# Low parts of plain weights by a negated copy and an adding transfer

## The chip, the cores and the metric

The kernel runs on one core of a Trainium2 chip. The metric is the time of one execution on the device in microseconds (us). The engines are TensorE (PE, matmuls; its weight loads are listed as PEld), VectorE (DVE), ScalarE (ACT), GpSimd (POOL) and SyncE (SP), which here issues nearly all transfers between the chip's memory and the core.

## The reference

Two layers of a diffusion trunk over 128 context and 512 latent tokens, 640 columns in all, of width 1024. A layer is a feed-forward network (FFN), a mixer, and a second FFN, each behind a normalization that is scaled and shifted by a conditioning vector:

```python
def ffn_sublayer(x, mod, k, g, w_in, w_out):
    h = modulated_norm(x, mod, k, g)
    gt, up = jnp.split(h @ w_in, 2, axis=-1)
    return x + 0.5 * mod[:, None, 3 * k + 2] * ((jax.nn.silu(gt) * up) @ w_out)

def trunk_layer(x, mod, ...):
    x = ffn_sublayer(x, mod, 0, norm_g[0], w_ffn_in[0], w_ffn_out[0])
    h = modulated_norm(x, mod, 1, norm_g[1])
    ...  # h @ w_in, then attention, pooling and convolution groups
    x = x + mod[:, None, 5] * y
    return ffn_sublayer(x, mod, 2, norm_g[2], w_ffn_in[1], w_ffn_out[1]), k, v
```

An FFN's hidden width is 2816, so w_in has 2 x 2816 columns. The conditioning values come from one product of each layer, 1024 by 9216, with the weights w_ada. All is in float32.

## The kernel before

The activations lie with the 1024 features on partitions (eight tiles x_92 to x_99 of 128 by 640) and are worked on in two halves of 320 columns. A float32 product is made of three products in a faster format (f32r): each operand is split into a high part, which is the value rounded to that format, and a low part, which is the rest. The function mm3 (L343 to L349) multiplies wh by xh (L347), wh by xl (L348) and wl by xh (L349).

A weight tile goes through these steps. SyncE loads it into one of five raw tiles (raw, 128 by 1024; L176). ScalarE copies it to wh, which rounds it (L170). Another engine subtracts wh from raw and writes wl (L171). Both are done by split_w; its argument eng says who subtracts: GpSimd, unless the caller names VectorE. There are four wh and four wl tiles of 1024 columns, and two of 512. A raw tile is free again when wh and wl have been made of it, and SyncE's queue waits for that before it issues the next load into it.

GpSimd makes the low parts of 330 tiles: 209 of 1024 columns (w_ffn_in, w_in, w_out and part of w_ffn_out), 64 of 640 (w_ffn_out) and 57 of 512. VectorE makes those of 114 sums of weight tiles, and of the first two tiles of the kernel.

The FFNs work through 22 column blocks of the gate and up weights. In the first FFN all are plain. In each of the other three the last 19 blocks, 57 in all, are done by fast_ups: seven half products in place of eight, with sums of raw tiles made by VectorE (`add`, L641). Of such a step's tiles, the up weights (1024 columns) and half of the gate weights (512 columns) go through GpSimd, and the two sums through VectorE. ScalarE keeps partial products (part, L666), applies silu (L677, L681) and copies the high part of g (L155); VectorE makes the low part of g (L156). The down products run in five chunks between the blocks and update x (L513, VectorE). Behind each FFN or mixer, squares of x are taken by ScalarE (sq, L246), added by VectorE (ssq, L247), and a matmul with ones sums them over the partitions (mis, L370). In three of the four FFNs the conditioning weights of the next stages are loaded through the same raw tiles (L150) and used by VectorE (L306) or TensorE (L270).

The order in which each engine takes its instructions is set by the program's scheduler, from its own estimates of durations; tiles are handed over by semaphores. The low part's subtraction is this one line, with h the high part:

```python
eng.tensor_tensor(lo, raw, f32(h), op=ALU.subtract)
```

Of the kernel before, what the change touches and what calls it, by code (L numbers as in the profile page):

```python
# [12 lines left out]
AF = mybir.ActivationFunctionType  # L13
ALU = mybir.AluOpType
# [82 lines left out]
def trunk_kernel(ctx: ExitStack, tc: tile.TileContext, i: dict, o: dict):  # L97
    nc = tc.nc
# [21 lines left out]
    def f32(ap):  # L120
        return ap.bitcast(F32)
# [42 lines left out]
    def split_w(raw, nk, width, eng=nc.gpsimd):  # L164

        view = lambda t: t[:, : nk * width].rearrange("p (k c) -> p k c", k=nk)
        size, tag = (1024, "") if nk * width > 512 else (512, "s")
        h = view(whp.tile([P, size], F32R, tag="wh" + tag, name="wh", bufs=4 if tag == "" else 2))
        lo = view(wlp.tile([P, size], F32R, tag="wl" + tag, name="wl", bufs=4 if tag == "" else 2))
        nc.scalar.activation(h, raw, AF.Copy)  # L170
        eng.tensor_tensor(lo, raw, f32(h), op=ALU.subtract)  # L171
        return h, lo

    def load_raw(src, c0, width=P, raw=None):
# [7 lines left out]
    def load_w(loads, nk=KD, width=P):  # L182
        return split_w(*raw_w(loads, nk, width))

    def load_cols(src, c0, width=P):
        return split_w(*load_raw(src, c0, width))
# [364 lines left out]
    def ffn(l, f, n, hs, side, finish, nxt, first=None):  # L551
# [83 lines left out]
        def fast_weights(j):  # L635

            nk = KD // 2
            up, *_ = load_raw(w_in, DFF + j * P)
            gate, *_ = load_raw(w_in, j * P)
            a1, a2, d1, d2 = up[:, :nk, :], up[:, nk:, :], gate[:, :nk, :], gate[:, nk:, :]  # L640
            add = lambda out, x, y: nc.vector.tensor_tensor(out, x, y, op=ALU.add)  # L641
            view = lambda t: t.rearrange("p (k c) -> p k c", k=KD)
            one, two = view(sum_tile()), view(sum_tile())
            ups = split_w(up, KD, P)
            add(one[:, :nk, :], a1, d1)
            add(one[:, nk:, :], d1, d2)
            add(two[:, :nk, :], one[:, nk:, :], a1)
            add(two[:, nk:, :], two[:, :nk, :], a2)
            late = split_w(d2, nk, P)
            twos = split_w(two, KD, P, nc.vector)  # L650
            ones = split_w(one, KD, P, nc.vector)
            first = lambda w: (w[0][:, :nk, :], w[1][:, :nk, :])
            second = lambda w: (w[0][:, nk:, :], w[1][:, nk:, :])
            return {1: first(ups), 2: second(ups), 3: second(twos), 4: late, 5: second(ones), 6: first(twos), 7: first(ones)}
# [731 lines left out]
```

## Time and profile before

| | us |
|---|---|
| median of three timed runs | 2446.3 (2445.64 to 2448.29) |
| the profiled execution | 2451.2 |
| its span | 2449.4 |
| TensorE busy in it | 2326.0 |
| VectorE, ScalarE, GpSimd busy | 1627.4, 952.9, 744.3 |

The mean granted clock of TensorE was 0.978 of the full one. The stages end at about 540 us (first FFN), 775 (mixer), 1275 (second FFN), 1750 and 1987 (the same of the second layer's first FFN and mixer), and 2449. Times inside a row are counted from the start of the span. Busy times of engines overlap, so they do not add up to the span; a wait of TensorE adds to it.

### The profile page before, as it was taken

Reading aid. Unit: us, or ns where it says so; the run is one execution under the profiler, and the core shown is the slowest. Engines: PE = TensorE matmul, PEld = TensorE weight load, DVE = VectorE, ACT = ScalarE, POOL = GpSimd, SP = SyncE. Lnnn points to the kernel's source line nnn. Section 1 sums busy time; section 2 is a strip of 40 time slices with the busy share of each in tenths; the row PEclk is TensorE's granted clock in tenths of the full one; section 3 lists DMA queues with packets and bytes.
Section 4 is the critical chain, followed back from the end, with each engine's and each line's share of the span. In section 5 each row is a group of like instructions: output and inputs, shape, how many; then the busy total and the mean of one; then the engine's idle time right before and its main releaser. Section 6 shows DMA issues by size and latency. Waiting matters only on the chain.

```text
span 2449.4 us, 40825 instructions
## 1 busy us (share of the span) xinstructions
PE 2326.0 (95%) x16594; PEld 2235.4 (91%) x16594; DVE 1627.4 (66%) x2907; ACT 952.9 (39%) x1750; POOL 744.3 (30%) x383
## 2 busy tenths in 40 slices
PE   7999999989899999999989999999898989999999
PEld 6999999979877899999989999999797789999998
DVE  5757776567868757466568475575778687566673
ACT  4322221234466424343335342343444564344351
POOL 2434333333311332232322323323242133332331
PEclk9999999989999999999999999999899999999999
DMA  8535454322211444353423333333122012322221
GB/s 264 155 112 166 145 166 128 122 70 69 62 35 35 127 124 123 111 164 98 135 70 98 110 117 108 121 110 108 52 80 59 27 44 67 91 84 78 78 87 44
DMA packets 341300, 247.57 MB, mean 101 GB/s; under 512 B 25752, under 2 KB 301560, under 8 KB 341112
## 3 DMA queue, kind: packets, MB, share of 16 engines
q1 hardware_dynamic: 340932, 244.88, 33.4%
q8 instruction: 131, 2.15, 0.4%
q14 instruction: 57, 0.47, 0.1%
q10 hardware_dynamic: 180, 0.07, 0.0%
HBM read 242.04 MB, written 2.88 MB: 100 GB/s over the span
## 4 chain that ended last, share of the span: by engine, by line
PE 74%; DVE 15%; DMA 4%; ACT 3%; issue 3%; POOL 0%; ACTq 0%; SPq 0%; DVEq 0%; POOLq 0%
PE acc L347 22%; PE acc L348 21%; PE acc L349 21%; DMA raw<-in_w_ffn_in 4%; DVE sums L641 3%; DVE sums L306 2%; PE mis L270 2%; DVE ssq L247 2%; PE po L1095 1%; DVE x L513 1%; PE acc L1055 1%; PE po L349 1%; PE po L348 1%; PE mis L1106 1%; PE po L347 1%
## 5 line engine op out<-in xcount | busy, mean ns | idle before, releaser
L171 POOL TENSOR_TENSOR wl<-raw,wh 128x1024 fp32r<-128x1024 f32 (+2 forms) x330 | 715.0, 2173 | 1594.0 <-ACT wh L170 1527.6
L347 PE MATMUL acc<-h,wh 128*128 128x320 f32 (+1 forms) x2808 | 881.5, 316 | 40.0 <-ACT part L666 13.9
L348 PE MATMUL acc<-h,wh 128*128 128x320 f32 (+1 forms) x2808 | 874.8, 312 | 6.7 <-DVE h L407 3.9
L349 PE MATMUL acc<-h,wl 128*128 128x320 f32 (+1 forms) x2808 | 872.1, 311 | 0.0
L347 PEld LDWEIGHTS acc<-h,wh 128*128 128x128 f32 x2808 | 532.7, 190 | 60.8 <-ACT part L666 17.9
L170 ACT ACTIVATE wh<-raw 128x1024 fp32r<-128x1024 f32 (+2 forms) x332 | 306.4, 923 | 655.2 <-PE acc L348 483.4
L348 PEld LDWEIGHTS acc<-h,wh 128*128 128x128 f32 x2808 | 533.4, 190 | 9.7 <-DVE h L407 4.1
L349 PEld LDWEIGHTS acc<-h,wl 128*128 128x128 f32 x2808 | 533.1, 190 | 0.6 <-issue 0.6
L347 PE MATMUL acc<-g,wh 128*128 128x320 f32 x1408 | 438.9, 312 | 20.0 <-DVE x L513 20.0
L348 PE MATMUL acc<-g,wh 128*128 128x320 f32 x1408 | 437.7, 311 | 0.0
L349 PE MATMUL acc<-g,wl 128*128 128x320 f32 x1408 | 436.6, 310 | 0.0
L513 DVE SCALAR_TENSOR_TENSOR x<-acc,gate,x 128x128 f32<-128x128 f32 (+2 forms) x480 | 194.5, 434 | 258.5 <-PE acc L349 257.3
L347 PEld LDWEIGHTS acc<-g,wh 128*128 128x128 f32 x1408 | 265.8, 189 | 24.3 <-issue 11.6
L349 PEld LDWEIGHTS acc<-g,wl 128*128 128x128 f32 x1408 | 266.2, 189 | 0.2
L348 PEld LDWEIGHTS acc<-g,wh 128*128 128x128 f32 x1408 | 266.0, 189 | 0.3
L170 ACT ACTIVATE wh<-sums 128x1024 fp32r<-128x1024 f32 x114 | 120.3, 1056 | 159.6 <-PE acc L348 140.3
L156 DVE TENSOR_TENSOR g<-part,g 128x320 fp32r<-128x320 f32 x114 | 143.0, 1254 | 56.6 <-ACT g L155 56.3
L306 DVE SCALAR_TENSOR_TENSOR sums<-raw,c,sums 128x512 f32<-128x512 f32 x196 | 174.1, 945 | 9.4 <-DMA raw<-in_w_ada 9.3
L171 DVE TENSOR_TENSOR wl<-sums,wh 128x1024 fp32r<-128x1024 f32 x114 | 139.5, 1225 | 53.3 <-ACT wh L170 40.6
L641 DVE TENSOR_TENSOR sums<-raw 128x512 f32<-128x512 f32 x114 | 107.2, 975 | 55.1 <-DMA raw<-in_w_ffn_in 54.4
L641 DVE TENSOR_TENSOR sums<-sums,raw 128x512 f32<-128x512 f32 x114 | 97.2, 853 | 2.0
L347 PE MATMUL acc<-mix,wh 128*128 128x320 f32 x256 | 83.7, 327 | 13.2 <-DVE u L1021 12.7
(199 smaller groups left out, 2528.7 us busy)
## 6 DMA issues: line engine op xcount, KB each, us to landing
raw<-in_w_ffn_in SPq DMA_DIRECT2D x176, 512.0 KB, 4.0
raw<-in_w_ada SPq DMA_DIRECT2D x128, 512.0 KB, 3.8
raw<-in_w_ffn_out SPq DMA_DIRECT2D x48, 512.0 KB, 4.0
raw<-in_w_ffn_out SPq DMA_DIRECT2D x64, 320.0 KB, 3.3
raw<-in_w_in SPq DMA_DIRECT2D x20, 512.0 KB, 3.8
adaw<-in_w_ada SPq DMA_DIRECT2D x16, 512.0 KB, 10.5
raw<-in_w_in SPq DMA_DIRECT2D x16, 256.0 KB, 4.0
raw<-in_w_out SPq DMA_DIRECT2D x8, 512.0 KB, 3.5
```

Of the source, the lines that this page charges most:

```text
L156: nc.vector.tensor_tensor(lo, src, f32(h), op=ALU.subtract)
L170: nc.scalar.activation(h, raw, AF.Copy)
L171: eng.tensor_tensor(lo, raw, f32(h), op=ALU.subtract)
L247: nc.vector.tensor_tensor(ssq[:, c:e], ssq[:, c:e], sq[:, : e - c], op=ALU.add)
L270: last = nc.tensor.matmul(ps[32 * g : 32 * g + 32, 0:P], c2[:, 2 * q + k, :], r[:, k, g * P : (g + 1) * P], start=(q + k == 0), stop=(q + ...
L306: nc.vector.scalar_tensor_tensor(part[:, j, :], r[:, k, :], c, part[:, j, :], op0=ALU.mult, op1=ALU.add)
L347: nc.tensor.matmul(out, wh, xh, start=start, stop=False, skip_group_check=onto)
L348: nc.tensor.matmul(out, wh, xl, start=False, stop=False, skip_group_check=onto)
L349: return nc.tensor.matmul(out, wl, xh, start=False, stop=stop, skip_group_check=onto)
L513: nc.vector.scalar_tensor_tensor(xT[t][:, s:e], ps[:, s - a : e - a], gates[l][n][:, t, j : j + 1], xT[t][:, s:e], op0=ALU.mult, op1=ALU.add,)
L641: add = lambda out, x, y: nc.vector.tensor_tensor(out, x, y, op=ALU.add)
L1055: nc.tensor.matmul(ps[:, :w], qs[2 * c + m][:, g, self.qc], self.kk[x][:, g, :], start=(x == 0), stop=(x == 1),)
```

## The change

Where GpSimd made a low part, ScalarE now writes the negated high part into the low part's tile, and a transfer issued by GpSimd's queue adds the raw tile onto it: lo = -wh, then lo = lo + raw. The other callers, with VectorE, are as before. Five lines are added, so that the lines below L171 are numbered five higher in the changed kernel.

```diff
         h = view(whp.tile([P, size], F32R, tag="wh" + tag, name="wh", bufs=4 if tag == "" else 2))
         lo = view(wlp.tile([P, size], F32R, tag="wl" + tag, name="wl", bufs=4 if tag == "" else 2))
         nc.scalar.activation(h, raw, AF.Copy)
-        eng.tensor_tensor(lo, raw, f32(h), op=ALU.subtract)
+        if eng is nc.gpsimd:
+
+            nc.scalar.activation(lo, f32(h), AF.Copy, scale=-1.0)
+            eng.dma_start(lo, raw, accum_op=ALU.add)
+        else:
+            eng.tensor_tensor(lo, raw, f32(h), op=ALU.subtract)
         return h, lo
```

It takes 330 subtractions from GpSimd, and adds 330 copies to ScalarE and 330 transfers from on-chip memory to on-chip memory. The scheduler orders the rest anew. Two places of ScalarE's queue show it. The first is the end of the first FFN, where the squares of the last tiles of x (x_93 to x_99) stand between copies of weights for the mixer. Before:

```order
L170 ACTIVATE wh<-raw 128x1024
L246 ACTIVATE sq<-x_93 128x320
L246 ACTIVATE sq<-x_94 128x320
L170 ACTIVATE wh<-raw 128x1024
L246 ACTIVATE sq<-x_95 128x320
L246 ACTIVATE sq<-x_96 128x320
L170 ACTIVATE wh<-raw 128x1024
L246 ACTIVATE sq<-x_97 128x320
L246 ACTIVATE sq<-x_98 128x320
L170 ACTIVATE wh<-raw 128x1024
L246 ACTIVATE sq<-x_99 128x320
L356 ACTIVATE r_5379<-mis,eps 128x320
```

After, from the second of these copies on:

```order
L170 ACTIVATE wh<-raw 128x1024
L251 ACTIVATE sq<-x_95 128x320
L173 ACTIVATE wl<-wh 128x1024
L251 ACTIVATE sq<-x_96 128x320
L170 ACTIVATE wh<-raw 128x1024
L251 ACTIVATE sq<-x_97 128x320
L173 ACTIVATE wl<-wh 128x1024
L251 ACTIVATE sq<-x_98 128x320
L170 ACTIVATE wh<-raw 128x1024
L251 ACTIVATE sq<-x_99 128x320
L173 ACTIVATE wl<-wh 128x1024
L361 ACTIVATE r_5449<-mis,eps 128x320
```

A copy now stands between any two squares, and a negated copy behind the last of them. The second place is a fast step of the third FFN (the one that begins near 1645 us before). Its up weights are raw_16891 before and raw_16968 after, its half of the gate weights raw_16893 and raw_16970. Before:

```order
L170 ACTIVATE wh_16766<-sums_16748 128x1024
L666 ACTIVATE part_16721<-acc_16619 128x320
L677 ACTIVATE part_16721<-part_16721 128x320
L666 ACTIVATE part_16785<-acc_16770 128x320
L170 ACTIVATE wh_16897<-raw_16891 128x1024
L155 ACTIVATE g_16811<-part_16721 128x320
L170 ACTIVATE wh_16905<-raw_16893 128x512
L681 ACTIVATE part_16682<-part_16682 128x320
L155 ACTIVATE g_16811<-part_16682 128x320
L666 ACTIVATE part_16833<-acc_16770 128x320
```

After:

```order
L170 ACTIVATE wh_16839<-sums_16819 128x1024
L671 ACTIVATE part_16797<-acc_16695 128x320
L671 ACTIVATE part_16858<-acc_16843 128x320
L682 ACTIVATE part_16797<-part_16797 128x320
L170 ACTIVATE wh_16974<-raw_16968 128x1024
L155 ACTIVATE g_16884<-part_16797 128x320
L173 ACTIVATE wl_16975<-wh_16974 128x1024
L170 ACTIVATE wh_16983<-raw_16970 128x512
L686 ACTIVATE part_16758<-part_16758 128x320
L173 ACTIVATE wl_16984<-wh_16983 128x512
L671 ACTIVATE part_16906<-acc_16843 128x320
L155 ACTIVATE g_16884<-part_16758 128x320
```

The negated copy of the up weights stands behind the high part of g, and that of the gate weights behind a silu; the next kept part (the second last row) now comes after both.

## Rows read from the trace of the kernel before

**Rows 1.** Page, busy time by engine, and the chain that ended last by engine.

```profile
PE 2326.0 (95%) x16594; PEld 2235.4 (91%) x16594; DVE 1627.4 (66%) x2907; ACT 952.9 (39%) x1750; POOL 744.3 (30%) x383
...
PE 74%; DVE 15%; DMA 4%; ACT 3%; issue 3%; POOL 0%; ACTq 0%; SPq 0%; DVEq 0%; POOLq 0%
```

**Rows 2.** Waits of TensorE: waited for, total us, times, longest us.

```profile
PE acc L347 <- DVE x L513: 23.7, 15, 4.1
PE mis L370 <- DVE ssq L247: 22.4, 5, 8.4
PE acc L347 <- ACT part L666: 13.9, 10, 3.1
PE acc L347 <- DVE u L1021: 12.7, 2, 6.4
```

**Rows 3.** Groups of instructions by shape, GpSimd: count | busy us, mean ns | idle before.

```profile
L171 POOL TENSOR_TENSOR wl<-raw,wh 128x1024 fp32r<-128x1024 f32 x209 | 519.5, 2487 | 1287.6 <-ACT wh L170 1230.8 <-PE acc L349 28.2 <-PE acc L1055 22.4
L171 POOL TENSOR_TENSOR wl<-raw,wh 128x640 fp32r<-128x640 f32 x64 | 102.1, 1596 | 248.5 <-ACT wh L170 248.5
L171 POOL TENSOR_TENSOR wl<-raw,wh 128x512 fp32r<-128x512 f32 x57 | 95.2, 1671 | 57.9 <-ACT wh L170 48.2 <-DVE g L156 9.5
```

**Rows 4.** Groups of instructions by shape, ScalarE, copies of high parts.

```profile
L170 ACT ACTIVATE wh<-raw 128x1024 fp32r<-128x1024 f32 x211 | 223.2, 1059 | 426.6 <-PE acc L348 314.9 <-issue 94.0 <-DMA raw<-in_w_ffn_in 11.0
...
L170 ACT ACTIVATE wh<-raw 128x640 fp32r<-128x640 f32 x64 | 47.3, 740 | 197.3 <-PE acc L348 160.6 <-PE acc L349 14.9 <-issue 12.7
L170 ACT ACTIVATE wh<-raw 128x512 fp32r<-128x512 f32 x57 | 35.9, 629 | 31.2 <-DMA raw<-in_w_ffn_in 21.2 <-PE acc L348 7.9 <-issue 2.0
```

**Rows 5.** Timeline, VectorE, end of the first FFN: start us, duration us, instruction.

```profile
527.22 0.49 DVE L247 TENSOR_TENSOR ssq<-ssq,sq 128x320 f32<-128x320 f32 x1
...
538.30 2.13 DVE L247 TENSOR_TENSOR ssq<-ssq,sq 128x320 f32<-128x320 f32 x1 [0.59 <-ACT sq L246]
```

**Rows 6.** Timeline, GpSimd, same place.

```profile
537.74 2.34 POOL L171 TENSOR_TENSOR wl<-raw,wh 128x1024 fp32r<-128x1024 f32 x1 [2.40 <-ACT wh L170]
```

**Rows 7.** Timeline, TensorE: last product, next matmul; the latter in the second layer.

```profile
531.76 0.31 PE L349 MATMUL acc<-g,wl 128*128 128x320 f32 x1
...
540.48 1.44 PE L370 MATMUL mis<-ssq,ones 128*128 128x320 f32 x2 [8.41 <-DVE ssq L247]
...
1750.58 1.43 PE L370 MATMUL mis<-ssq,ones 128*128 128x320 f32 x2 [8.30 <-DVE ssq L247]
```

**Rows 8.** Stretches: length, busy us (count) by engine, granted clock, DMA share, GB/s.

```profile
545.00:550.00 5.00, 5.00 (x25) 5.00 (x25) 5.00 (x18) 3.06 (x8) 0.00 (x0) 0.66 0.03 11
550.00:560.00 10.00, 10.00 (x70) 10.00 (x70) 8.81 (x24) 6.24 (x14) 0.00 (x0) 1.00 0.00 0
```

**Rows 9.** DMA issues: count, KB each, median us to landing.

```profile
raw<-in_w_ffn_in SPq DMA_DIRECT2D x176, 512.0 KB, 4.0
...
raw<-in_w_ffn_out SPq DMA_DIRECT2D x64, 320.0 KB, 3.3
...
adaw<-in_w_ada SPq DMA_DIRECT2D x16, 512.0 KB, 10.5
```

**Rows 10.** Timeline, ScalarE, fast step of the third FFN, up weights.

```profile
1645.26 1.06 ACT L170 ACTIVATE wh<-raw 128x1024 fp32r<-128x1024 f32 x1
```

**Rows 11.** Timeline, TensorE, first product with that tile's low part.

```profile
1655.52 0.31 PE L349 MATMUL acc<-h,wl 128*128 128x320 f32 x1
```

**Rows 12.** Timeline, ScalarE, fast step of the last FFN, up weights.

```profile
2236.50 1.07 ACT L170 ACTIVATE wh<-raw 128x1024 fp32r<-128x1024 f32 x1 [0.24 <-PE acc L348]
```

**Rows 13.** Timeline, TensorE, first product with that tile's low part.

```profile
2245.55 0.31 PE L349 MATMUL acc<-h,wl 128*128 128x320 f32 x1
```

**Rows 14.** Waits of VectorE.

```profile
DVE sums L641 <- DMA raw<-in_w_ffn_in: 54.4, 29, 3.9
```

**Rows 15.** Timeline, VectorE, low parts of g in the step of rows 10.

```profile
1646.94 2.22 DVE L156 TENSOR_TENSOR g<-part,g 128x320 fp32r<-128x320 f32 x1 [0.54 <-ACT g L155]
...
1651.20 0.49 DVE L156 TENSOR_TENSOR g<-part,g 128x320 fp32r<-128x320 f32 x1 [0.54 <-ACT g L155]
```

## The prediction

> **What bounds the kernel now.** I read the page first, then the waits of TensorE, then the stretches in which it waited longest, then the DMA issues, and last the fast steps of the three later FFNs, where the changed weights are most numerous. The page shows TensorE busy for 95% of the span and holding 74% of the chain of waits; VectorE (DVE) has 15% of that chain, ScalarE 3%, and GpSimd none [rows 1]. So GpSimd's 744 us of work are worth nothing by themselves. What a change off TensorE can win is inside its idle time, and the largest entries of that are four: updates of x, sums of squares, kept partial products, and the mixer's u [rows 2]. Two of the five waits for sums of squares are long, and they stand at the end of the first FFN of each layer. In the first one the last product ends near 532.07 and the next matmul begins at 540.48, after 8.41 us; in the second, near 1750, it is 8.30 us [rows 7]. In that gap a sum of squares takes 2.13 us, whereas the same operation took 0.49 us a little earlier [rows 5], and the long one lies beside a subtraction of GpSimd that began 0.6 us before it and ended 0.35 us before it [rows 6]. The reader is to see there that VectorE, with two operands in on-chip memory, stood still until GpSimd was done. The same is seen in the fast steps: one low part of g took 2.22 us beside a subtraction and 0.49 us without one [rows 15]. There TensorE has other products to do, and does not wait.
>
> **What goes.** The 330 subtractions of 2.49, 1.60 and 1.67 us [rows 3] go, and with them the stretching of VectorE.
> - The two long waits [rows 7]: after the last product there remain the update of x, the square on ScalarE, the sum of 0.49 us and the matmul's start. The first two go over the same 320 columns as the sum, so I take 0.5 us for each of the three and some 0.8 for handing over, 2.3 us in all and 6 us less than now, each time: 12 us.
> - The other three waits for sums of squares hold 22.4 - 16.7 = 5.7 us [rows 2]; I take 4 of them.
> - In the five microseconds behind the long gap the granted clock was 0.66 on average, between the levels of 1.2 and 2.4 GHz, after TensorE had idled, and 25 matmuls were done; the next ten, at the full clock, held 70 [rows 8], 35 in five. So 10 x 0.143 = 1.4 us are lost each time; with a short gap I take them as won, 3 us for two.
> - The mixer's two waits for u have 12.7 us, and the fifteen for x 23.7 [rows 2]. VectorE is partly stretched there too; I take 3 and 2 us.
> The gains are 24 us. Everything else that VectorE wins lies beside products.
>
> **What comes in its place: copies on ScalarE.** A negated copy reads and writes what the copy of the high part does, so I price it by that: 209 x 1.059 + 64 x 0.740 + 57 x 0.629 = 305 us [rows 3, 4]. That brings ScalarE from 953 to 1258 us, 51% of the span [rows 1]. Beside it TensorE works; but ScalarE is waited for 13.9 us at kept parts [rows 2], and a longer queue makes these waits longer. In proportion to its load they grow by 13.9 x 305/953 = 4.4 us. At the ends of the FFNs the order of ScalarE now has one copy between any two squares; none stands after the last but one more negated copy, so I charge nothing more there (one copy each, 2 us, if the last square is caught behind it).
>
> **What comes in its place: 330 adding transfers.** The trace has no transfer within on-chip memory and none that adds. The nearest rows bound it: a load of 512 KB lands 4.0 us after its issue, one of 320 KB after 3.3, and the slowest kind, sixteen of 512 KB in a row, after 10.5 [rows 9]. The first two give a slope of 0.7 us for 192 KB, so 1.9 us for the bytes of a large tile and 2.1 us that do not depend on them. An adding transfer must read the raw tile and the tile it adds onto; I count its bytes twice, 2.1 + 2 x 1.9 = 5.9 us. GpSimd, which issues the transfer, is held up by VectorE in the fast steps: its subtractions of 512 columns, which stand only there, took 1.67 us, though those of 640 took 1.60 [rows 3], so 1.67 - 1.60 x 0.8 = 0.39 us more than their size asks. I add this as an allowance and take 6.3 us for a large tile, between 4.0 and 10.5, nearer to the lower end as the loads that are spaced like these transfers are there.
>
> The Trainium skill, "Collectives: The Full Stack", section "The bandwidth ceiling: the fold count and why AG ≠ RS ≠ AR", states that a transfer that reduces is slower than a copy not through its addition but through its second source, which passes through the same read ring and doubles the traffic. By it the data part is paid twice, 5.9 us; without it 4.0, and rival 1 below would lose half of its chance. No run here shows it yet.
>
> What hides it: in a fast step of the second layer's first FFN the copy of the high part ends at 1646.32 [rows 10], and the first product that needs the low part starts at 1655.52 [rows 11] (which matmul uses which tile I found by counting the products in program order). Of these 9.20 us the new order spends some 0.5 on the high part of g and 1.06 on the negated copy, and 0.1 on handing over: 7.5 us are left for the transfer. The 38 fast steps of two FFNs look like this. In the last FFN, where no modulation work lies between the products, the copy ends at 2237.57 [rows 12] and the use is at 2245.55 [rows 13]: 7.98 - 1.6 = 6.4 us, in 19 steps. At 6.3 us neither waits. The low parts of the down products and of the plain steps have at least as much, worked out in the same way.
>
> Where the lead is shorter than the new chain, TensorE pays. A low part is ready 1.06 + 6.3 - 2.49 = 4.9 us later than now. At the kernel's start and at the start of an FFN the weights have little lead; there I charge one such delay, 5 us in sum (0 to 15, if three places pay it in full).
>
> A raw tile is given back when the transfer has landed, also 4.9 us later, and SyncE's queue issues its loads in order, many of them after waiting for exactly this release. VectorE already waits 54.4 us in 29 places for a raw tile's landing [rows 14]; it would wait longer there, with the parts of the step queued behind that wait, but has 2 us fewer of stretched work in the same step [rows 15]. I set the one against the other and count zero, with bounds of -12 (the relief is used) and +40 us (about 1.4 us at each of the 29 places reach TensorE).
>
> **The sum.** 24 won, 4.4 + 5 paid: 14.6 us less than the profiled execution's 2451.2 us, 2436.6. That execution is 4.9 us above the median of the three timed runs, 2446.3, so the forecast is 2431.7, say 2431 us. A difference under 0.2% of the time, 5 us, cannot be told from no change in this kernel.
>
> **Rivals.**
> 1. The transfer lands too late (slower). It decides from 6.4 us on in 19 steps and from 7.5 on in 38. For it: the 10.5 us of loads that queue behind each other, and that GpSimd and VectorE exclude one another [rows 5, 6]. Against it: a fast step issues only two such transfers. At 9 us: 1.5 x 38 + 2.6 x 19 = 106 us, so 2431 + 106 = 2537 us; at 10.5: 3 x 38 + 4.1 x 19 = 192, 2623 us.
> 2. The issue waits for VectorE. If GpSimd is held up at each transfer as long as a sum of squares was by it, 2.13 - 0.49 = 1.64 us [rows 5] in place of 0.39, the transfer takes 7.5 us: 1.1 x 19 = 21 us, and 2452 us, no change or a little slower. The Trainium skill, "SBUF — State Buffer", section "SBUF: two separate sides", describes this as a trap: a transfer issued from GpSimd needs its descriptors written by GpSimd's cores, and a VectorE operation that takes the shared port pair keeps them out; it reports 3.1 us where 0.62 were normal. By that sentence, an estimate, 2.5 us more than 5.9 would make 8.4 us, some 70 us of waits and 2501 us. The trace agrees that the two engines exclude each other, 2.13 against 0.49 us, but shows no descriptor being written.
> 3. Late raw tiles. The 40 us of the bound above come, and the gains stay: 2431 + 40 = 2471 us. For it speak the 29 places; against it, that what VectorE makes of these tiles is needed only by products of the step after, so that only what is queued behind its wait can suffer.
> 4. The relief is hidden: squares wait behind ScalarE's copies at the ends in place of GpSimd's subtractions, 2 us at each of five waits and nothing won at x and u, which leaves some 24 - 15 - 9 = 0: 2446 us.
>
> **How the numbers follow.** The forecast has 0.46; its own range is 2410 (gains of 40, as VectorE also uses its relief in the fast steps) to 2441. Rival 1 has 0.27, rival 2 0.08, rival 3 0.11, rival 4 0.08. Faster is the forecast's 0.46 and a little of the fourth, 0.47; within 0.2% is most of the fourth and a third of the second, 0.10; slower is the rest, 0.43. The range for all must leave out no more than 2 in 10: from 2410 up to 2560, which holds rival 1 up to about 9.4 us a transfer.
>
> **What the changed profile would show.** Right: sums of squares of 0.5 us throughout, waits of TensorE for them under 3 us at the FFNs' ends with no clock below 1.0 for long after; VectorE's busy time well below 1627 us; ScalarE near 1258 us; transfers landing in 5 to 7 us; no wait of a product for a low part in the fast steps. Wrong: waits of TensorE's line for the low part's matmul (L354 after) on a transfer, some 1 to 4 us in each of 19 or 57 steps; or SyncE's loads issued so late that ScalarE and VectorE wait hundreds of microseconds for raw tiles, and through their queues TensorE at kept parts.

## The result: slower by 0.9%, the gains were there and the bodies lost more

The changed kernel takes 2466.8 us (median of five runs, 2460.5 to 2474.7) against 2446.3 for the kernel before in the same rounds; the ratio is 1.0089, with an interval of 1.0063 to 1.0115. The forecast of 2431 us had the wrong sign. The third rival had 2471 us. One execution of mix_raw6 and one of mix_raw7, two of the experiments below, took 12348.9 and 5738.8 us; their ratios leave these out.

The page of the changed kernel: busy time by engine, then the transfers' queues (packets, MB, share of the 16 engines' span), then the issues (count, KB each, median us to landing).

```profile
PE 2341.6 (95%) x16594; PEld 2250.0 (91%) x16594; DVE 1324.6 (54%) x2907; ACT 1217.4 (49%) x2080; POOL 317.4 (13%) x383
...
q1 hardware_dynamic: 340932, 244.88, 32.9%
q0 software_dynamic: 47520, 145.51, 32.7%
...
wl<-raw POOLq DMA_DIRECT2D x209, 512.0 KB, 5.2
raw<-in_w_ffn_in SPq DMA_DIRECT2D x176, 512.0 KB, 5.0
raw<-in_w_ada SPq DMA_DIRECT2D x128, 512.0 KB, 5.2
...
raw<-in_w_ffn_out SPq DMA_DIRECT2D x64, 320.0 KB, 4.2
wl<-raw POOLq DMA_DIRECT2D x64, 320.0 KB, 4.5
```

VectorE lost 303 us of work and ScalarE gained 264 [rows 1]. An adding transfer of 512 KB landed after 5.2 us, sooner than the 6.3 taken. But the queue of these transfers takes as large a share of the DMA engines (32.7%) as all loads (32.9%), and a load of 512 KB of w_ffn_in now lands after 5.0 us and not 4.0, one of 320 KB after 4.2 and not 3.3 [rows 9].

What TensorE waits for in the changed kernel (total us, times, longest):

```profile
PE acc L352 <- DVE x L518: 41.5, 13, 6.9
PE acc L352 <- ACT part L671: 24.5, 17, 3.3
PE acc L354 <- DMA wl<-raw: 15.4, 13, 4.7
...
PE mis L375 <- DVE ssq L252: 3.8, 2, 1.9
...
PE acc L352 <- DVE u L1026: 1.3, 2, 0.7
```

Against [rows 2], the sums of squares fell from 22.4 to 3.8 us and u from 12.7 to 1.3; the updates of x rose from 23.7 to 41.5, kept parts from 13.9 to 24.5, and 15.4 us for low parts are new.

Where the time went is told best by stage. Each normalization begins with a matmul that sums squares (L370, after L375), once for each half of the tokens; I cut both traces at these starts, and call the piece between the two halves an end. In us:

| | first FFN | end | mixer | end | FFN 2 | end | FFN 3 | end | mixer | end | FFN 4 | four bodies | ends and mixers |
|---|---|---|---|---|---|---|---|---|---|---|---|---|---|
| before | 519.1 | 21.4 | 219.2 | 24.5 | 474.3 | 22.5 | 448.2 | 21.4 | 220.6 | 24.5 | 453.7 | 1895.3 | 554.1 |
| after | 530.3 | 14.9 | 209.7 | 17.2 | 494.3 | 17.2 | 481.7 | 14.8 | 212.4 | 17.1 | 463.4 | 1969.6 | 503.3 |

So the ends and mixers became 51 us shorter, and the FFN bodies 74 us longer; the profiled execution, 2474.7 us, is the longest of the five.

The end of the first FFN, in the changed kernel; VectorE, then TensorE (start us, duration us, instruction, and in brackets the idle time before it and what ended it):

```profile
541.08 0.49 DVE L252 TENSOR_TENSOR ssq<-ssq,sq 128x320 f32<-128x320 f32 x1 [0.76 <-ACT sq L251]
...
544.60 0.49 DVE L252 TENSOR_TENSOR ssq<-ssq,sq 128x320 f32<-128x320 f32 x1 [0.75 <-ACT sq L251]
```

```profile
542.95 0.31 PE L354 MATMUL acc<-g,wl 128*128 128x320 f32 x1
...
545.15 1.40 PE L375 MATMUL mis<-ssq,ones 128*128 128x320 f32 x2 [1.89 <-DVE ssq L252]
```

This answers to [rows 5, 7]: no sum of squares takes more than 0.5 us, and the gap is 1.89 us in place of 8.41. The clock did not gain by it here. In the second five microseconds after that matmul, read as [rows 8], TensorE does 19 matmuls at a granted clock of 0.50, the level of 1.2 GHz; before, behind the long gap, it did 25 at 0.66:

```profile
550.00:555.00 5.00, 4.86 (x19) 4.46 (x18) 5.00 (x18) 3.29 (x9) 0.62 (x2) 0.50 1.00 239
```

The low parts of g have lost their stretch as well; all 114 in the fast steps before, then after (us in sum, mean ns of one):

```profile
L156 DVE TENSOR_TENSOR g<-part,g 128x320 fp32r<-128x320 f32 x114 | 143.0, 1254 | 56.6 <-ACT g L155 56.3
```

```profile
L156 DVE TENSOR_TENSOR g<-part,g 128x320 fp32r<-128x320 f32 x114 | 56.0, 492 | 68.5 <-ACT g L155 67.6
```

The loss is seen in a down stage of the third FFN. First SyncE's queue, GpSimd and ScalarE, then VectorE, then TensorE:

```profile
1595.86 1.88 SPq L181 DMA_DIRECT2D raw<-in_w_ffn_in  x2
```

```profile
1598.19 0.89 POOL L174 DMA_DIRECT2D wl<-raw  x1 [2.69 <-ACT part L682]
```

```profile
1604.04 0.63 ACT L170 ACTIVATE wh<-raw 128x512 fp32r<-128x512 f32 x1 [5.90 <-DMA raw<-in_w_ffn_in]
```

```profile
1598.24 0.67 DVE L518 SCALAR_TENSOR_TENSOR x<-acc,gate,x 128x128 f32<-128x128 f32 x2 [0.88 <-PE acc L354]
1604.11 0.69 DVE L646 TENSOR_TENSOR sums<-raw 128x512 f32<-128x512 f32 x1 [5.20 <-DMA raw<-in_w_ffn_in]
1604.72 0.54 DVE L518 SCALAR_TENSOR_TENSOR x<-acc,gate,x 128x320 f32<-128x320 f32 x1
```

```profile
1605.32 0.42 PE L352 MATMUL acc<-g,wh 128*128 128x320 f32 x1 [3.61 <-DVE x L518]
```

Two loads go out from 1595.86 on, an adding transfer at 1598.19; the loads are in at about 1604, after some 8 us. The 16 DMA engines are full meanwhile: their share (the last number but one; the one before it is the granted clock) is over 1.

```profile
1601.00:1606.00 5.00, 1.39 (x9) 1.13 (x9) 1.85 (x4) 1.26 (x2) 0.26 (x1) 1.00 1.12 264
```

VectorE stands at a sum of raw tiles for 5.20 us, with the update of x behind it in its queue, and TensorE waits 3.61 us for that update, since it frees the accumulator. The wait costs more than its length, as the granted clock is lower after it:

```profile
1606.00:1611.00 5.00, 5.00 (x26) 5.00 (x25) 2.63 (x7) 2.11 (x2) 1.47 (x2) 0.66 0.87 244
```

26 matmuls are done in these five microseconds at a granted clock of 0.66, between the levels of 1.2 and 2.4 GHz; 35 are done at the full one [rows 8]. Over the whole kernel TensorE's busy time rose from 2326.0 to 2341.6 us, for the same 16594 matmuls.

SyncE's queue, which waited for GpSimd's subtractions before it could load into a raw tile, now waits for the landings of adding transfers (before, then after; total us, times, longest):

```profile
SPq L176 <- POOL wl L171: 997.8, 205, 38.3
```

```profile
SPq L181 <- DMA wl<-raw: 1353.4, 222, 37.0
```

And the waits for raw tiles grew over the whole kernel, VectorE's from 54.4 us [rows 14] to the first of these rows, ScalarE's from 32.2 [rows 4] to the second:

```profile
DVE sums L646 <- DMA raw<-in_w_ffn_in: 167.0, 37, 7.8
```

```profile
ACT wh L170 <- DMA raw<-in_w_ffn_in: 178.9, 38, 12.4
```

### The profile page after: what moved, and what is told of

The parts are those of the page before. It is cut to its first block, busy times and chain, and to the rows that moved or that the text cites. A ratio compares the mean times of both kernels' runs of the same rounds, so it can differ in the third digit from the quotient of the medians.

```text
span 2472.9 us, 41585 instructions
## 1 busy us (share of the span) xinstructions
PE 2341.6 (95%) x16594; PEld 2250.0 (91%) x16594; DVE 1324.6 (54%) x2907; ACT 1217.4 (49%) x2080; POOL 317.4 (13%) x383
## 3 DMA queue, kind: packets, MB, share of 16 engines
q1 hardware_dynamic: 340932, 244.88, 32.9%
q0 software_dynamic: 47520, 145.51, 32.7%
## 4 chain that ended last, share of the span: by engine, by line
PE 55%; issue 19%; DMA 16%; DVE 5%; ACT 3%; POOL 1%; POOLq 0%; ACTq 0%; SPq 0%; DVEq 0%
PE acc L352 16%; PE acc L353 16%; PE acc L354 16%; DMA wl<-raw 7%; DMA raw<-in_w_ffn_in 7%; POOL wl L174 1%; PE mis L275 1%; DMA raw<-in_w_ada 1%; DVE sums L646 1%; ACT wl L173 1%; PE acc L1060 1%; PE po L352 1%; PE mis L1111 1%; PE po L353 1%; PE po L354 1%
## 5 line engine op out<-in xcount | busy, mean ns | idle before, releaser
L352 PE MATMUL acc<-h,wh 128*128 128x320 f32 (+1 forms) x2808 | 886.4, 318 | 59.1 <-ACT part L671 24.5
L354 PE MATMUL acc<-h,wl 128*128 128x320 f32 (+1 forms) x2808 | 875.9, 313 | 15.5 <-DMA wl<-raw 15.4
L174 POOL DMA_DIRECT2D wl<-raw x330 | 287.7, 872 | 2049.3 <-ACT wl L173 1425.5
L352 PE MATMUL acc<-g,wh 128*128 128x320 f32 x1408 | 444.1, 315 | 33.5 <-DVE x L518 33.5
L353 PE MATMUL acc<-g,wh 128*128 128x320 f32 x1408 | 442.1, 314 | 0.0
L173 ACT ACTIVATE wl<-wh 128x1024 fp32r<-128x1024 f32 (+2 forms) x330 | 302.6, 917 | 4.7
L352 PEld LDWEIGHTS acc<-g,wh 128*128 128x128 f32 x1408 | 270.4, 192 | 37.9 <-DVE x L518 26.3
L353 PEld LDWEIGHTS acc<-g,wh 128*128 128x128 f32 x1408 | 270.6, 192 | 0.3
L646 DVE TENSOR_TENSOR sums<-raw 128x512 f32<-128x512 f32 x114 | 74.7, 688 | 167.5 <-DMA raw<-in_w_ffn_in 167.0
L311 DVE SCALAR_TENSOR_TENSOR sums<-raw,c,sums 128x512 f32<-128x512 f32 x196 | 134.7, 744 | 38.3 <-DMA raw<-in_w_ada 38.3
L671 ACT ACTIVATE part<-acc 128x320 f32<-128x320 f32 x171 | 72.9, 426 | 42.5 <-PE acc L354 42.4
L156 DVE TENSOR_TENSOR g<-part,g 128x320 fp32r<-128x320 f32 x114 | 56.0, 492 | 68.5 <-ACT g L155 67.6
```

Of the source, the lines that this page charges most:

```text
L156: nc.vector.tensor_tensor(lo, src, f32(h), op=ALU.subtract)
L173: nc.scalar.activation(lo, f32(h), AF.Copy, scale=-1.0)
L174: eng.dma_start(lo, raw, accum_op=ALU.add)
L311: nc.vector.scalar_tensor_tensor(part[:, j, :], r[:, k, :], c, part[:, j, :], op0=ALU.mult, op1=ALU.add)
L352: nc.tensor.matmul(out, wh, xh, start=start, stop=False, skip_group_check=onto)
L353: nc.tensor.matmul(out, wh, xl, start=False, stop=False, skip_group_check=onto)
```

## Experiments

The theory from these traces (theory 1): adding transfers give raw tiles back late and slow the loads, so the next raw tiles land late, and what is queued behind them on VectorE and ScalarE reaches TensorE late. Paired copy by copy, the time from the end of ScalarE's copy to the end of the raw tile's last reader (the release, for short) is 2.48 us in the median before and 6.5 in the FFN bodies after. Its rivals: ScalarE's 305 us of copies (theory 2), and low parts that land too late (theory 3). The kernel before ran beside all of these at 2450.9 to 2451.4 us, so ratios are compared, and differences between experiments are given in us.

**Gain and loss apart.** mix_dma keeps the change for the mixers and the first two blocks of the later FFNs; ffn_dma is its complement.

```diff
+    adding = [True]
-        if eng is nc.gpsimd:
+        if eng is nc.gpsimd and adding[0]:
...
     def ffn(l, f, n, hs, side, finish, nxt, first=None):
+        adding[0] = False
...
+            adding[0] = True
             ups_by_half(0, 2)
+            adding[0] = False
...
     def mixer(l, hs, finish, nxt):
+        adding[0] = True
```

> Negated copy and adding transfer only for the mixers' weights and for the first two column blocks of the three later FFNs; all other plain low parts are subtracted on GpSimd as before. By the traces of before and after, the ends of the FFNs and mixers and the mixers themselves became 52 us shorter and the FFN bodies 72 us longer. If the two are separate, this kernel keeps the first and drops the second: 2446 - 52 = 2394 us, between 2390 and 2405. If the shorter ends were only work shifted between stages, so that the bodies pay for them, 2440 us or more.

> The complement: adding transfers only inside the FFNs (from the third block on, and the whole first FFN), subtraction on GpSimd for the mixers and the first two blocks. If gain and loss are separate: 2446 + 72 = 2518 us, 2505 to 2525. If they are not, near the changed kernel's 2467.

mix_dma took 2408.2 us, 0.9824 (0.9809 to 0.9840); ffn_dma 2518.4 us, 1.0263 (1.0246 to 1.0281). The two add up: -43 and +67 us give +24, where the changed kernel, by its ratio, has +22. By stage, mix_dma has 505.6 us of ends and mixers and 1900.7 us of bodies, ffn_dma 555.2 and 1966.2. The gain is real and separate, and lies in the first; the loss, but for 5 us, in the second. The gain came out 9 us short of the expectation. Part of the loss is the clock: ffn_dma's profiled span is 72 us longer than before's, and 28 us of that are longer busy time of TensorE for the same matmuls (2326.0 us before), at a mean granted clock of 0.968 in place of 0.978:

```profile
PE 2354.1 (93%) x16594; PEld 2257.7 (90%) x16594; DVE 1399.7 (56%) x2907; ACT 1167.4 (46%) x2024; POOL 405.6 (16%) x383
```

**ScalarE's copies.** neg_pool keeps them, and GpSimd adds.

```diff
-            eng.dma_start(lo, raw, accum_op=ALU.add)
+            eng.tensor_tensor(lo, raw, f32(lo), op=ALU.add)
```

> ScalarE's negated copies stay, 330 of them, but GpSimd adds the raw tile itself in place of a transfer. Theory 1 (raw tiles come back late and their loads land late, since transfers hold them and share the DMA engines): the loss in the FFN bodies is gone, and GpSimd's lock on VectorE is back, so 2446 to 2460 us. Theory 2 (305 us more copies on ScalarE delay the kept parts): the loss of about 72 us stays without the gain at the ends, 2500 to 2520 us. Theory 3 (low parts land late): as theory 1.

2464.2 us, 1.0054 (1.0042 to 1.0066): 13 us, 15 in the bodies, and 4 us more than theories 1 and 3 allowed. Theory 2 is out as the main cause: TensorE waited 9.7 us for kept parts, less than the 13.9 before. Part of the 13 us may again be the raw tile, which here is free 3.6 us after the copy (median, bodies) and not 2.5; that part was not measured.

**One more raw tile.** The changed kernel with six.

```diff
-    rawp = pool("raw", 5)
+    rawp = pool("raw", 6)
...
-    slots = pool("slots", 22)
+    slots = pool("slots", 21)
```

> The changed kernel with six raw tiles in place of five (and 21 in place of 22 tiles of the activations' pool, to make room). Theory 1: a load starts one tile earlier, and much of the loss in the FFN bodies goes: 2425 to 2450 us. If the loss is by the transfers' share of the DMA engines alone, so that loads are slow whenever they start, or theory 2 or 3: 2460 to 2475 us.

2440.6 us, 0.9953 (0.9939 to 0.9968): against the changed kernel's 1.0089 that is 1.4% or 33 us less. Loads that can start earlier give back about half of the loss. Whether they land late because they start late or because they are slow, this does not say: an earlier start helps against both. VectorE's wait for raw tiles fell to

```profile
DVE sums L646 <- DMA raw<-in_w_ffn_in: 131.6, 30, 7.1
```

while TensorE's wait for low parts did not fall (18.6 us, from 15.4), so theory 3 has no more than these to explain.

**Release without traffic, traffic without release.** All on top of mix_dma. hold: a transfer of 2 KB also reads the raw tile. traffic: transfers of about the tile's size, two for a large one, read the high part instead, and add it onto a spare tile; nothing waits for the result but the next transfer onto the same spare tile. mix_slots21: the control for the room that traffic needs.

```diff
             eng.tensor_tensor(lo, raw, f32(h), op=ALU.subtract)
+            if eng is nc.gpsimd:   # hold
+                eng.dma_start(tiny[len(drops) % 4], raw[:, 0, 0:4], accum_op=ALU.add)
...
+                    for x in range(2):   # traffic, a tile of 1024 columns
+                        eng.dma_start(spare[x], f32(whole(h))[:, x * 512 : x * 512 + 512], accum_op=ALU.add)
```

> On top of mix_dma (2408 us): in the FFN bodies, where GpSimd subtracts, a transfer of 2 KB that reads the raw tile follows each subtraction, so that the raw tile comes back some 3 us later, with next to no traffic. The adding transfers gave it back about 1.06 + 5.2 - 2.5 = 3.8 us later and cost the bodies 67 us. If the late release is the larger cause: 2440 to 2460 us. If the transfers' traffic is, which slows the loads: 2405 to 2420 us.

> On top of mix_slots21: in the FFN bodies a transfer (two for a large tile) of about the bytes of the weight tile adds the high part onto a spare tile, which nothing waits for; the raw tile comes back as soon as GpSimd has subtracted. If the traffic is the larger cause of the 67 us: 2440 to 2475 us. If the late release is: 2405 to 2425 us. Loads should land in about 5 us in place of 4.0 under both.

> mix_dma with 21 in place of 22 tiles of the activations' pool, the control for the kernels that need the room: 2408 us, 2403 to 2414.

mix_slots21 took 2407.5 us, 0.9821 (0.9801 to 0.9841): no effect. hold took 2560.2 us, 1.0443 (1.0420 to 1.0465), 152 more than mix_dma and outside every expectation. It did not test what it should: nothing tied the small transfer behind the subtraction, the scheduler put it ahead, and GpSimd's queue stood at it until the raw tile had landed:

```profile
POOL tiny L182 <- DMA raw<-in_w_ffn_in: 529.5, 122, 14.1
```

traffic took 2501.7 us, 1.0208 (1.0182 to 1.0234): 94 us more than mix_slots21 and 27 more than the highest that was expected, with the release as before (2.48 us in the median) and its loads at

```profile
raw<-in_w_ffn_in SPq DMA_DIRECT2D x176, 512.0 KB, 5.5
```

So the kernel loses without any later release. That all of the 94 us are the slower loads is not shown, as traffic also gives GpSimd two issues for a large tile, and GpSimd stood 74.0 us at spare tiles. hold2 mends hold, and issue_only is its control: the same small transfers, which read the high part.

```diff
+            low = eng.tensor_tensor(lo, raw, f32(h), op=ALU.subtract)
+            if eng is nc.gpsimd:
+                with tc.issue_after(low.ins):   # hold2; issue_only reads f32(h) in place of raw
+                    eng.dma_start(tiny[len(drops) % 4], raw[:, 0, 0:4], accum_op=ALU.add)
```

> As hold, on top of mix_dma (2408 us), but each transfer of 2 KB from the raw tile is issued behind its subtraction; in hold the scheduler had put it ahead, where it blocked GpSimd's queue until the raw tile had landed. The raw tile now comes back about 0.9 + 2.1 = 3.0 us later, and the loads stay at 4.0 us. If the late release alone costs, and in proportion: 67 x 3.0 / 4.2 = 48 us, 2456 us. If the traffic's slowing of loads is the cause (traffic: loads 5.5 us, 94 us lost with the release as before): 2410 to 2425 us.

> hold2 with the transfers of 2 KB reading the high part's tile in place of the raw tile: the same transfers and issues on GpSimd, but the raw tile is free once it is subtracted. If hold2's 47 us are the raw tile's late release: 2408 to 2420 us here. If they are the issues on GpSimd (some 0.9 us each, ahead of the next subtraction): 2440 to 2458 us.

hold2 took 2454.7 us, 1.0017 (1.0003 to 1.0031), 47 more than mix_dma, as the release theory had said; but issue_only took 2428.5 us, 0.9905 (0.9890 to 0.9920), 20 more, where it gave at most 12. So 20 us of the 47 come with the small transfers whatever they read, first of all with their issues on GpSimd, 0.95 us each, and 26 with the late release, which was 2.0 us (4.45 us after the copy in the median in place of 2.48). VectorE's waits for raw tiles show it, in hold2 and then in issue_only:

```profile
DVE sums L655 <- DMA raw<-in_w_ffn_in: 88.1, 34, 5.2
```

```profile
DVE sums L655 <- DMA raw<-in_w_ffn_in: 49.9, 29, 3.9
```

The loads took as long in both, 3.9 us. In hold2:

```profile
raw<-in_w_ffn_in SPq DMA_DIRECT2D x176, 512.0 KB, 3.9
...
tiny<-raw POOLq DMA_DIRECT2D x274, 2.0 KB, 2.0
```

traffic1 is traffic with one transfer for a tile.

```diff
+                with tc.issue_after(low.ins):
+                    eng.dma_start(spare[x], f32(whole(h))[:, : min(n, 448 if n == 512 else n)], accum_op=ALU.add)
```

> traffic with one transfer for a tile, of the size and row length of the changed kernel's, in place of two halves for a large one (20 activation tiles make the room). If the loads' slowing alone costs about what the rest of the 67 us is beside the release: 2420 to 2445 us, with loads near 5 us. If it still costs 80 us or more, the two causes overlap in the changed kernel and cannot be added: 2485 us or more.

2488.4 us, 1.0153 (1.0129 to 1.0178): 80 us more than mix_dma, 60 more than issue_only, which has its issues. Its loads and transfers:

```profile
raw<-in_w_ffn_in SPq DMA_DIRECT2D x176, 512.0 KB, 5.4
spare<-wh POOLq DMA_DIRECT2D x153, 512.0 KB, 6.7
```

GpSimd also stood 107 us at spare tiles whose last transfer had not landed, so a part of the 60 may be that. Another part may be the room: traffic1 has 20 activation tiles in place of 22, which no run with five raw tiles controls, and of the 56 us between the two profiled executions 47 lie in the bodies and 9 in the mixers, where it has no such transfers. In issue_only, traffic and traffic1 no copy of ScalarE waited for such a transfer to let go of a high part's tile. Neither expectation fits whole: it is above the first and at the edge of the second. Late release costs 26 us for 2.0 us, and traffic up to 60 us for loads that land 1.5 us later; in the changed kernel the release is some 4 us later and the loads 1.0 us, and the bodies lose 67 to 74 us. The parts don't add up exactly, and needn't: in the experiments GpSimd's subtractions still hold up VectorE in the bodies, in the changed kernel they don't. How many microseconds that relief gives back there was not measured. Nor was it measured what the scheduler's new order, which differs from kernel to kernel, is worth by itself.

**Which transfers of the bodies.** On top of mix_dma, adding transfers for the fast steps' weights alone (mix_fast) or for the down weights alone (mix_down).

```diff
+            adding[0] = True   # mix_fast; mix_down has the same around load_cols in down()
             ups = split_w(up, KD, P)
...
             late = split_w(d2, nk, P)
+            adding[0] = False
```

> On top of mix_dma (2408 us), adding transfers also for the up and half gate weights of the 57 fast steps. In the profile of the changed kernel VectorE's longest waits for raw tiles stood in the down stages, where loads, down weights and adding transfers meet. If the fast steps' own transfers cost little: 2410 to 2425 us; if they carry half of the 67 us: 2435 to 2450 us.

> On top of mix_dma (2408 us), adding transfers also for the down weights of the chunks between the blocks. If the meeting in the down stages carries the loss: 2435 to 2460 us; if the fast steps do: 2410 to 2420 us.

2426.6 us, 0.9898 (0.9883 to 0.9913), and 2432.1 us, 0.9919 (0.9900 to 0.9938): 18 and 24 us, by their waits through different doors. With the fast steps' transfers TensorE waits for kept parts, with those of the down weights for updates of x (mix_fast, then mix_down; in mix_dma 12.2 us were for kept parts and 19.5 for x):

```profile
PE acc L353 <- ACT part L675: 25.9, 15, 3.4
PE acc L353 <- DVE x L519: 14.3, 12, 3.5
```

```profile
PE acc L353 <- DVE x L519: 36.4, 20, 7.1
PE acc L353 <- ACT part L675: 12.2, 10, 2.2
```

mix_down fell below its expectation by 3 us, and mix_fast lies 2 us above the lower of its two; neither kind carries the loss alone, and the other 25 us of the 67 are, if the parts add up, with the plain blocks (the first FFN's and the third block of the others), the last chunks, or the two together.

**The version that beats both.** mix_dma with six or seven raw tiles.

> mix_dma with six raw tiles and 21 activation tiles. The sixth raw tile gave the changed kernel 26 us. If it only repairs the late release of the adding transfers, it gives nothing here, as the FFN bodies subtract on GpSimd: 2403 to 2413 us. If loads were late for the bodies before the change too: 2390 to 2403 us.

> mix_dma with seven raw tiles and 20 activation tiles; six gave 2399 us. If the loads' lead still binds: 2385 to 2395 us; if the sixth was enough, or 20 activation tiles make the blocks wait: 2397 us or more.

Six took 2398.9 us, 0.9780 (0.9764 to 0.9796), 9 us less than mix_slots21, so loads were a little late for the bodies before the change too; seven 2397.7 us, 0.9778 (0.9763 to 0.9793), no more.

## Why the prediction was wrong

- What bounds the kernel, and VectorE's stretching: right. The rows of the ends read as they should, and the stretch is gone everywhere.
- The gains: right in kind, half in size. 24 us were forecast, 43 (mix_dma) to 51 us (by stage) came. The two FFN ends gave 6.5 us each where 6 were said. The mixers and the ends behind them gave 32 us of the 51, where the sum had held 3 for u and part of 4 for the other sums of squares: u alone won 11.4. I took a quarter of waits that stood at work of VectorE with two operands, beside GpSimd's subtractions, as the long ones did. The 3 us of the clock were not won: behind the first FFN's end 19 matmuls were done where 25 had been, and in the like stretch behind the third's 24, at 0.73, where 20 had been, at 0.50.
- ScalarE's copies: 305 us forecast, 302.6 measured at L173 (ScalarE's busy time rose by 264, as copies overlap with what was there). Their price of 4.4 us stands against 13 in neg_pool, which also has a later release.
- The adding transfer: 6.3 us forecast, 5.2 measured, and the cover in the fast steps held: TensorE waited 15.4 us for low parts in all, in 13 places, mostly at the starts of the kernel and of its stages, where the sum had charged 5. The 5.9 us of bytes paid twice was nearer than the 4.0 of a plain load before; but plain loads beside these transfers landed after 5.0. Rivals 1 and 2, which needed more than 6.4 us, fell with this. Whether the second source doubles the traffic, as the Trainium skill has it for a transfer that reduces ("Collectives: The Full Stack", section "The bandwidth ceiling: the fold count and why AG ≠ RS ≠ AR"), is left open by it: 5.2 lies between the two.
- The failed step is the raw tile's release, "I set the one against the other and count zero, with bounds of -12 [...] and +40 us". It was +67. The release came 4 us later, about as said (4.9), but three things were missing. The sum had the transfer wait for loads and never loads for the transfer: 145 MB of adding transfers beside 245 MB of loads took as much of the DMA engines as the loads do, and most loads landed 0.9 to 1.4 us later ([rows 9], and w_ada's from 3.8 to 5.2). traffic1 shows what that costs without a later release, at most 60 us. The relief of VectorE cannot pay for a wait at the head of its queue: an engine with less work stands just as long at a tile that has not landed. hold2 against issue_only shows 26 us for 2 us of lateness alone. And the bound gave these waits their length alone, 1.4 us at 29 places, and nothing for the lower clock after them; TensorE's longer busy time made up 28 of the 72 us of ffn_dma's longer span. The prediction's own sign of being wrong, hundreds of microseconds of waits for raw tiles on ScalarE and VectorE, did come: 178.9 and 167.0 us.
- Rival 3 had the right mechanism and nearly the right time, 2471 us for 2466.8, partly by luck: its loss was 27 us too small, and so were the gains under it.
- The reason given against it was that VectorE's sums are needed only a step later, "so that only what is queued behind its wait can suffer". That was so, and it was enough, as the down stage above shows: what reached TensorE late was the x update queued behind the sum, not the sum.

## To carry to other kernels

Before work is moved from an engine to the DMA engines, count its bytes against what the DMA engines already move, and price every load as landing later; a tile's release and its reload are one chain, and a wait at the head of an in-order queue is not paid by making that queue's other work shorter. A trick that loses over a whole kernel can still win where its cover is free: here 56 of 330 tiles, in the stages with few loads, bring 1.8%. A wait of TensorE can cost more than its length: behind the 3.61 us of the down stage 26 matmuls were done in the time of 35.

## What the runs showed of the hardware

- An adding transfer of 512 KB within on-chip memory landed in 5.2 us, one of 320 KB in 4.5, one of 256 KB in 4.7 (medians of the changed kernel): between these sizes the bytes matter little. One of 2 KB took 2.0 us from a raw tile (hold2) and 4.0 from a high part's tile (issue_only); what makes these two differ is open.
- The issue of an adding transfer occupied GpSimd for 0.87 us. 274 issues of 2 KB between subtractions, 0.95 us each, came with 20 us for the kernel although no computation needed their result (issue_only, where GpSimd also stood 13.7 us until earlier ones had landed).
- A transfers' queue of 32.7% share lengthened the loads of another queue from 4.0 to 5.0 us, although the 16 engines were busy two thirds of the time in the mean; in the down stage above they were full. In traffic, whose raw tiles came back as before, such loads took 5.5 us.
- Beside GpSimd's subtractions the low parts of g took 1254 ns of VectorE in the mean, without them 492.
